# Gate rows: transposed on TensorE and sent in runs of 512 bytes, instead of scattered in runs of 4 bytes

## The chip, the cores and the metric

One core of a Trainium2 chip runs the kernel. The metric is the device time of one execution in microseconds (us). Three runs of the kernel before took 2084.08, 2084.61 and 2075.7 us, median 2084.08.

Engines: PE is TensorE (matmuls; PEld its weight loads), DVE VectorE, ACT ScalarE, POOL GpSimd, and SP the queue that issues all DMAs here.

## The reference

One decoder layer on x (256 tokens, 2048 features, float32), conditioned by one vector c of 2048.

```python
cond = silu(c)
sh1, sc1, gt1, sh2, sc2, gt2, sh3, sc3, gt3 = split(cond @ ada_w + ada_b, 9)
x = x + 0.5 * gt1 * swiglu(ada_in(x, norm_g[0], sh1, sc1), ...)      # FFN 1
x = x + gt2 * hybrid_mixer(ada_in(x, norm_g[1], sh2, sc2), ...)      # attention and delta-rule heads
x = x + 0.5 * gt3 * swiglu(ada_in(x, norm_g[2], sh3, sc3), ...)      # FFN 2
out = rmsnorm(x, final_norm)
```

`ada_in` is an RMS norm that is scaled and shifted by vectors of the nine. `swiglu(h) = (silu(h wg) * (h wu)) wd` with an inner width of 5632. The change touches only the three gate vectors `gt1`, `gt2`, `gt3` (2048 numbers each), on their way to where they multiply a row of x.

## The kernel before

**Weights.** All weight matrices are packed on the host into 5392 tiles of 128x128, in the order in which they are used, and read in 674 blocks of eight tiles (512 KB). In this text the blocks are counted from 0 in that order. For each block SP issues a load into `wraw` (L98), ACT casts it to `whi` (L100, the high part of a split of float32 into two), DVE subtracts to get `wlo` (L116, the low part), and PE multiplies with both. There are three buffers of each in the mixer, and one more of each (`more`, for every fourth block) in the FFNs. Loads therefore run ahead of casts, and casts ahead of PE, by as many blocks as there are buffers.

**Stages.** FFN 1 uses blocks 0 to 263 (gate and up projections of the first 28 of 44 column groups from block 0, their down projection from block 112, then the second part), the mixer blocks 264 to about 410, FFN 2 the rest. In a gate/up step PE accumulates into PSUM pairs `pgu`, DVE multiplies the two halves (`sg`, or `acc` in the first part), PE transposes the product (`pz`, L554, eight transposes) and ACT and DVE split it into `hid`. In a down step PE accumulates into `pd`, and `residual` (L498, L499) multiplies it with the gate row `gtr` (as `rs`) and adds it to x.

**The vectors of the conditioning.** The nine vectors are not computed by matmuls. Each column group of 128 outputs is one load of 1 MB (`adat`, L251) and one DVE instruction that multiplies it with silu(c) and sums along the row (L262, 2.35 us), into one column of the tile `mod` (128 x 160). So vector m lies in `mod` as 16 columns: number p of group j is at partition p, column 16 m + j. A table of paces (`RATE`) says how many of these sums go with each weight block.

**Gate rows.** The residual needs the gate vector along the free axis and on all partitions: `gtr`, 128 x 2048, every partition the same. Each gate vector (m = 2, 5 and 8) goes there by quarters of 512 numbers, b = 0 to 3, in two steps that are queued as soon as the fourth column of a quarter is summed (in `ada_sum`):
- `row_send` (L294): a DMA from four columns of `mod` to the DRAM tile `gd`;
- `row_load` (L300): a DMA from `gd` to all partitions of a quarter of `gtr`.

`W.after(n, f)` runs f when the program is written out n weight blocks later. With `ROW_LAG = (6, 13)` the send follows the sum by 6 blocks and the load by 13. Both wait in program order behind the newest weight load (`issue_after(W.last)`). There is one `gtr` for three gates, so a row of the next gate may be loaded only after the last residual of the current one: `gate["open"]` names the current one. Sums of gate 5 that are done while gate 2 is open queue nothing; when FFN 1 is written out, `gate_open(5)` queues all four sends 6 blocks later and all four loads 13 blocks later. `row_need` forces what is still owed before a residual. `bank` (used for `pgu`, `pd`, `pz`) hands out the eight PSUM banks in turn.

**What sets the order.** The program is written in the order of the weight blocks; a scheduler then orders each engine's instructions by its own estimate of when they become ready, so an added instruction can move others. Each engine and SP's queue run their instructions strictly in that order: what waits holds up what stands behind it.

Of the kernel before, what the change touches and what calls it, by code (L numbers as in the profile page):

```python
# [8 lines left out]
F32 = mybir.dt.float32  # L9
# [7 lines left out]
P = 128  # L17
D = 2048
T = 256
KD = D // P  # L20
# [8 lines left out]
ROW_LAG = (6, 13)  # L29
# [101 lines left out]
def layer_kernel(ctx: ExitStack, tc: tile.TileContext, xrow, c, adaw, cols, cst, fng, w, out, order, dbg=None):  # L131
    nc = tc.nc
    V, A, G, PE = nc.vector, nc.scalar, nc.gpsimd, nc.tensor
# [7 lines left out]
    tiny = ctx.enter_context(tc.tile_pool(name="tiny", bufs=2))  # L141
# [13 lines left out]
    def psn(i, name):  # L155

        i %= 8
        return psb(name) if i < N_BIG else pss(name) if i < N_BIG + N_GDN else psf(name)

    W = Stream(nc, w, raw, hi, lo)  # L160
# [10 lines left out]
    gdram = ctx.enter_context(tc.tile_pool(name="gdram", bufs=1, space=bass.MemoryType.DRAM)).tile([3, KD, P], F32, name="gd")  # L171
# [47 lines left out]
    def L(name, lo_=0, n=None):  # L219
        o, wd = COL[name]  # L220
        return colt[:, o + lo_ : o + (wd if n is None else lo_ + n)]

    ident = L("ident")

    mod = keep.tile([P, 10 * KD], F32, name="mod")
# [7 lines left out]
    def ada_col():  # L233

        i = ada_st["i"]
        if i >= len(ada_seq):
            return
        ada_st["i"] += 1
        m, j = ada_seq[i]
        if first_ada:  # L240
            t = first_ada.pop(0)
            if i >= 2:
                with tc.issue_after(W.last):
                    nc.sync.dma_start(t, adaw[i])
        else:
            t = adap.tile([P, D], F32, name="adat")
            if W.last is None:
                nc.sync.dma_start(t, adaw[i])
            else:
                with tc.issue_after(W.last):  # L250
                    nc.sync.dma_start(t, adaw[i])  # L251
        ada_open.append(lambda: ada_sum(t, m, j))
        if i < 2 * KD:
            ada_close(i)
        else:
            W.after(ADA_LAG, lambda: ada_close(i))

    def ada_sum(t, m, j):

        q = m * KD + j  # L260
        with W.behind(False):
            V.tensor_tensor_reduce(t, t, cs, HALF.get(m, 1.0), L("adab", q, 1), ALU.mult, ALU.add, mod[:, q : q + 1])  # L262
        if (m, j) in ada_done:
            ada_done[m, j]()
        if m in ROW and j % 4 == 3:
            row_owed[m, j // 4] = [row_send, row_load]
            if m == gate["open"]:
                row_soon(m, j // 4)

    def ada_close(i):  # L270

# [4 lines left out]
    ROW = {2: 0, 5: 1, 8: 2}  # L276
    row_owed, gate = {}, {"open": 2}

    def row_soon(m, b):

        for n in ROW_LAG:
            W.after(n, lambda: row_next(m, b))

    def gate_open(m):

        gate["open"] = m
        for e, b in row_owed:
            if e == m:
                row_soon(m, b)

    def row_send(m, b):

        with tc.issue_after(W.last):
            nc.sync.dma_start(gdram[ROW[m], 4 * b : 4 * b + 4].rearrange("j p -> p j"), mod[:, m * KD + 4 * b : m * KD + 4 * b + 4])  # L294

    def row_load(m, b):

# [1 line left out]
        with tc.issue_after(W.last):  # L299
            nc.sync.dma_start(gtr[:, 512 * b : 512 * b + 512], src)  # L300

    def row_next(m, b):

        if row_owed.get((m, b)):
            row_owed[m, b].pop(0)(m, b)

    def row_need(m, b):

        ada_need(m, 4 * b + 3)
        while row_owed[m, b]:  # L310
            row_next(m, b)
# [202 lines left out]
    def bank(name):  # L514

        turn[0] += 1
        return psn(turn[0], name)
# [123 lines left out]
    def ffn(which, m_sh, m_sc, m_gt, squares):  # L641
        f_ = PARTS[which]
        with tc.tile_pool(name=f"hid{which}", bufs=f_[1] // 4) as hp, \
                (nullcontext(sp_0) if which == 0 else tc.tile_pool(name=f"sg{which}", bufs=2)) as sp, \
                tc.tile_pool(name=f"more{which}", bufs=1) as more:
            W.more = (more, more, more) if MORE else None
            for half in range(2):
                if which == 0 and half == 0:
                    r = first_row
                    for j in range(KD):  # L650
                        ada_done[0, j] = lambda j=j: modulate_one(j, gains(0, 1, j, 1), mod[:, j : j + 1], r)
                    W.hold, W.held = None, [ada_done[0, 0]().ins]
                    chunks, lead, need = list(zip(CHUNKS[:-1], CHUNKS[1:])), LEAD, lambda k: ada_need(0, k)
                else:
                    if half == 0:
                        modulate(2 * which, m_sh, m_sc, hview[0])
                    chunks, lead, need = [(0, KD)], (LATER_LEAD if half == 0 else 0,), h_need
                hid = gate_up(which, f_[half], f_[half + 1], hp, sp, chunks, lead, need)
                if half and squares == "final":
                    fng_load()  # L660
                down(which, f_[half], f_[half + 1], hid, m_gt, squares if half else None)
            W.more = None
        if which == 0:
            gate_open(5)
# [72 lines left out]
    def mixer():  # L737
# [488 lines left out]
        for bs in ((0, 1), (2,), (3,)):  # L1226
# [9 lines left out]
            else:  # L1236
                for t in range(2):
                    residual(pj[3][t], t, 3, 5, "mid")
        gate_open(8)
        mx.close()  # L1240

# [131 lines left out]
```

## Time and profile before

| | |
|---|---|
| runs, us | 2084.08, 2084.61, 2075.7 |
| profiled execution, us | 2079.78 (its span 2078.0) |
| mean granted TensorE clock | 0.982 |
| FFN 1 | 0 to 784 us |
| mixer | 784 to 1320 us |
| FFN 2 and the final norm | 1320 to 2078 us |
| moved by DMA | 524.20 MB, 251 GB/s over the span |

How to read the rows below. A timeline row is: start in us from the span's start, duration, engine, line of the kernel, operation, tiles out<-in, shapes, count, and in brackets the idle time before it and what ended it. `SPq` is SP's queue; its duration is the issue, not the transfer. A matmul's own row lasts 0.39 us, but they are pipelined, 0.22 to 0.23 us apart at full clock. A row of a stretch is: from:to and its length, busy time (and instructions) of PE, PEld, DVE, ACT and POOL, the granted TensorE clock, the busy share of the DMA engines (over 1 where transfers overlap in an engine), and the GB/s moved. A wait row is: who <- whom, us in total, times, longest.

### The profile page before, as it was taken

The numbers are of one execution on the slowest core, as the hardware profiler recorded it, in microseconds if no ns is written. First come the engines' busy times: TensorE is split into PE (matmuls) and PEld (weight loads), VectorE is DVE, ScalarE is ACT, GpSimd is POOL, SyncE is SP. The second block draws the span as 40 slices with busy tenths as digits, with TensorE's granted clock in tenths as the row PEclk, the third lists the DMA queues.
The fourth block names the chain that finished last, engine by engine and source line by source line (L and its number), as shares of the span: only waits on it lengthen the run. The fifth ranks groups of instructions, "written<-read, shape, count | busy, mean of one in ns | idle before, by whom it ended". The sixth has DMA issues, their size and how long they took to land.

```text
span 2078.0 us, 25410 instructions
## 1 busy us (share of the span) xinstructions
PE 2010.1 (97%) x9372; PEld 1653.0 (80%) x9373; DVE 1487.4 (72%) x2073; ACT 993.3 (48%) x1426; POOL 2.7 (0%) x15
## 2 busy tenths in 40 slices
PE   8999999999999998999999989989999999999997
PEld 6788878777888887788878878778888888888886
DVE  7999989887877877898868866755556554455454
ACT  6544444333334446856656644644444344444443
POOL 0000000000000000000000000000000000000000
PEclk9999999999999999999999989999999999999999
DMA  9989899987888885666565556667678765555653
GB/s 364 353 319 360 307 311 317 352 354 310 326 330 335 329 298 193 205 228 205 202 225 187 187 182 243 202 183 257 219 245 256 190 220 193 193 190 189 209 192 132
DMA packets 139455, 524.20 MB, mean 252 GB/s; under 512 B 24633, under 2 KB 29881, under 8 KB 121025
## 3 DMA queue, kind: packets, MB, share of 16 engines
q1 hardware_dynamic: 139330, 522.58, 72.3%
q8 instruction: 73, 1.20, 0.2%
q14 instruction: 52, 0.43, 0.1%
HBM read 517.10 MB, written 5.41 MB: 251 GB/s over the span
## 4 chain that ended last, share of the span: by engine, by line
PE 81%; DVE 7%; DMA 6%; ACT 3%; issue 2%; SPq 0%; ACTq 0%; DVEq 0%
PE pgu L532 14%; PE pgu L535 14%; PE pgu L533 14%; PE pd L535 7%; PE pd L532 7%; PE pd L533 7%; PE pp L476 5%; DVE wlo L116 3%; DMA wraw<-in_w_dram 3%; PE pp L477 2%; DMA adat<-in_ada_dram 2%; PE po L532 1%; PE po L535 1%; PE po L533 1%; DVE adat L262 1%
## 5 line engine op out<-in xcount | busy, mean ns | idle before, releaser
L100 ACT CAST whi<-wraw 128x1024 fp32r<-128x1024 f32 x674 | 705.8, 1053 | 867.6 <-DMA wraw<-in_w_dram 321.8
L116 DVE TENSOR_TENSOR wlo<-wraw,whi 128x1024 fp32r<-128x1024 f32 x674 | 815.2, 1222 | 385.1 <-ACT whi L100 382.6
L532 PE MATMUL pgu<-whi,hs 128*128 128x512 f32 x1408 | 552.4, 394 | 10.4 <-ACT hs L382 5.8
L533 PE MATMUL pgu<-whi,hs 128*128 128x512 f32 x1408 | 549.5, 391 | 2.2 <-DVE hs L427 2.2
L535 PE MATMUL pgu<-wlo,hs 128*128 128x512 f32 x1408 | 436.3, 391 | 4.2 <-DVE wlo L116 4.0
L262 DVE CUSTOM_DVE_ANT_0 adat<-adat,cs,colt 128x2048 f32<-128x2048 f32 x140 | 328.7, 2348 | 53.7 <-DMA adat<-in_ada_dram 53.1
L532 PEld LDWEIGHTS pgu<-whi,hs 128*128 128x128 f32 x1408 | 266.3, 189 | 68.0 <-ACT hs L382 6.7
L535 PEld LDWEIGHTS pgu<-wlo,hs 128*128 128x128 f32 x1408 | 264.2, 188 | 62.5 <-DVE wlo L116 8.0
L533 PEld LDWEIGHTS pgu<-whi,hs 128*128 128x128 f32 x1408 | 266.0, 189 | 58.0 <-DVE hs L427 2.7
L532 PE MATMUL pd<-whi,hid 128*128 128x512 f32 x704 | 275.8, 392 | 1.3 <-ACT whi L100 1.3
L533 PE MATMUL pd<-whi,hid 128*128 128x512 f32 x704 | 275.1, 391 | 0.0
L476 PE MATMUL pp<-hs,whi 128*128 128x512 f32 x656 | 241.9, 405 | 1.3 <-ACT xn L414 1.1
L535 PE MATMUL pd<-wlo,hid 128*128 128x512 f32 x704 | 224.8, 392 | 6.4 <-DVE wlo L116 6.2
L477 PE MATMUL pp<-hs,wlo 128*128 128x256 f32 x656 | 188.4, 287 | 0.9 <-DVE wlo L116 0.9
L535 PEld LDWEIGHTS pd<-wlo,hid 128*128 128x128 f32 x704 | 132.2, 189 | 36.8 <-DVE wlo L116 9.6
L532 PEld LDWEIGHTS pd<-whi,hid 128*128 128x128 f32 x704 | 133.0, 189 | 29.9 <-ACT whi L100 2.2
L533 PEld LDWEIGHTS pd<-whi,hid 128*128 128x128 f32 x704 | 132.9, 189 | 27.6
L476 PEld LDWEIGHTS pp<-hs,whi 128*128 128x128 f32 x656 | 124.8, 190 | 25.6 <-ACT xn L414 1.5
L477 PEld LDWEIGHTS pp<-hs,wlo 128*128 128x128 f32 x656 | 125.2, 191 | 2.3 <-DVE wlo L116 1.4
L788 PE MATMUL pv<-wlo,hs 128*128 128x512 f32 x128 | 52.0, 406 | 2.8 <-DVE wlo L116 2.8
L789 PE MATMUL pv<-whi,hs 128*128 128x512 f32 x128 | 51.4, 401 | 0.0
L787 PE MATMUL pv<-whi,hs 128*128 128x512 f32 x128 | 51.2, 404 | 0.0
(310 smaller groups left out, 1372.4 us busy)
## 6 DMA issues: line engine op xcount, KB each, us to landing
wraw<-in_w_dram SPq DMA_DIRECT2D x674, 512.0 KB, 4.4
adat<-in_ada_dram SPq DMA_DIRECT2D x140, 1024.0 KB, 7.6
gtr<-gd SPq DMA_DIRECT2D x12, 256.0 KB, 6.7
rw<-rowd SPq DMA_DIRECT2D x24, 128.0 KB, 4.0
x<-in_xr_dram SPq DMA_DIRECT2D x4, 512.0 KB, 6.0
adaf<-in_ada_dram SPq DMA_DIRECT2D x4, 512.0 KB, 7.9
adaf<-in_ada_dram SPq DMA_DIRECT2D x2, 1024.0 KB, 12.5
xd<-x SPq DMA_DIRECT2D x4, 512.0 KB, 7.0
```

Of the source, the lines that this page charges most:

```text
L100: self.cast = self.nc.scalar.copy(self.h, r).ins
L116: nc.vector.tensor_tensor(self.l, r, self.h.bitcast(F32), ALU.subtract)
L262: V.tensor_tensor_reduce(t, t, cs, HALF.get(m, 1.0), L("adab", q, 1), ALU.mult, ALU.add, mod[:, q : q + 1])
L476: PE.matmul(ps, wt[0], act.rearrange("p a t -> p (a t)"), start=first, stop=False)
L477: PE.matmul(ps[:, :T], wt[1], act[:, 0], start=False, stop=last)
L532: PE.matmul(ps[t], hi_(t), wh, start=first, stop=False)
L533: PE.matmul(ps[t], lo_(t), wh, start=False, stop=False)
L535: PE.matmul(ps[t], hi_(t), wl, start=False, stop=last)
L787: PE.matmul(pv[t], hs[:, k, 0, sl], wh, start=(k == 0), stop=False)
L788: PE.matmul(pv[t], hs[:, k, 0, sl], wl, start=False, stop=False)
L789: PE.matmul(pv[t], hs[:, k, 1, sl], wh, start=False, stop=(k == KD - 1))
```

## The change

- A quarter is now sent in three instructions instead of one: PE transposes the four columns of `mod` into a PSUM bank (`pgr`, 4 x 128), ACT copies that to a small tile `gs` (4 x 128), and SP sends `gs` to `gd`. The DMA writes four runs of 512 B instead of 512 runs of 4 B.
- The send is queued 6 blocks after the sum for every gate, open or not. So gate 5's four sends move from the start of the mixer into FFN 1.
- The load is queued 13 blocks after the sum where the gate is open, as before; where it opens later, at 2 + b blocks after `gate_open` instead of 13.

```diff
         if m in ROW and j % 4 == 3:
             row_owed[m, j // 4] = [row_send, row_load]
+            W.after(ROW_LAG[0], lambda: row_next(m, j // 4, 2))
             if m == gate["open"]:
-                row_soon(m, j // 4)
+                row_soon(m, j // 4, ROW_LAG[1])
...
-    def row_soon(m, b):
-
-        for n in ROW_LAG:
-            W.after(n, lambda: row_next(m, b))
+    def row_soon(m, b, n):
+
+        W.after(n, lambda: row_next(m, b, 1))
 
     def gate_open(m):
 
         gate["open"] = m
         for e, b in row_owed:
             if e == m:
-                row_soon(m, b)
+                row_soon(m, b, 2 + b)
 
     def row_send(m, b):
 
+        pg = bank("pgr")
+        PE.transpose(pg[:4, :P], mod[:, m * KD + 4 * b : m * KD + 4 * b + 4], ident)
+        gs = tiny.tile([4, P], F32, name="gs")
+        A.copy(gs, pg[:4, :P])
         with tc.issue_after(W.last):
-            nc.sync.dma_start(gdram[ROW[m], 4 * b : 4 * b + 4].rearrange("j p -> p j"), mod[:, m * KD + 4 * b : m * KD + 4 * b + 4])
+            nc.sync.dma_start(gdram[ROW[m], 4 * b : 4 * b + 4], gs)
...
-    def row_next(m, b):
-
-        if row_owed.get((m, b)):
+    def row_next(m, b, left=0):
+
+        while len(row_owed[m, b]) >= max(left, 1):
             row_owed[m, b].pop(0)(m, b)
+            if not left:
+                break
```

The added lines stand ahead of most of the kernel, so line numbers after them grow by up to 6 (L498 becomes L504).

Where the instructions stand. First SP's queue near the end of FFN 1, where weight loads 235 to 240 are issued; before:

```order
L98 DMA wraw_5317<-in_w_dram 128x1024
L98 DMA wraw_5335<-in_w_dram 128x1024
L251 DMA adat_5341<-in_ada_dram 128x2048
L98 DMA wraw_5355<-in_w_dram 128x1024
L98 DMA wraw_5374<-in_w_dram 128x1024
L98 DMA wraw_5392<-in_w_dram 128x1024
L251 DMA adat_5399<-in_ada_dram 128x2048
```

and now:

```order
L98 DMA wraw_5348<-in_w_dram 128x1024
L98 DMA wraw_5371<-in_w_dram 128x1024
L251 DMA adat_5377<-in_ada_dram 128x2048
L98 DMA wraw_5391<-in_w_dram 128x1024
L298 DMA gd_91<-gs_5356 4x128
L98 DMA wraw_5410<-in_w_dram 128x1024
L98 DMA wraw_5428<-in_w_dram 128x1024
L251 DMA adat_5435<-in_ada_dram 128x2048
```

Gate 5's fourth send now stands between weight loads 237 and 238. It reads `gs_5356`, which ACT writes at this place of its own order (now; casts 235 to 238):

```order
L100 CAST whi_5350<-wraw_5348 128x1024
L100 CAST whi_5373<-wraw_5371 128x1024
L296 COPY gs_5356<-pgr_5354 4x128
L100 CAST whi_5393<-wraw_5391 128x1024
L100 CAST whi_5412<-wraw_5410 128x1024
```

The copy stands behind cast 236; on PE its transpose stands behind the last matmul of block 234. The other sends are placed alike: counted in weight blocks, the transposes of FFN 1 stand behind blocks 83, 95, 106, 118 (gate 2), 200, 208, 216, 234 (gate 5), the copies behind casts 87, 98, 110, 121, 202, 209, 218, 236, and the sends behind loads 88, 99, 111, 121, 203, 214, 224, 237. In FFN 2 these are 431, 463, 495, 527, then four casts and seven loads later.

Last, DVE around block 127, where the first residual of FFN 1 stands; before:

```order
L116 TENSOR_TENSOR wlo_3097<-wraw_3093,whi_3095 128x1024
L498 TENSOR_TENSOR rs_3101<-pd_2802,gtr_87 128x512
L498 TENSOR_TENSOR rs_3124<-pd_2803,gtr_87 128x512
L499 TENSOR_TENSOR x_85<-x_85,rs_3101 128x512
L499 TENSOR_TENSOR x_85<-x_85,rs_3124 128x512
L262 ISA adat_3104,mod_137<-adat_3104,cs_86,colt_93 128x2048
L262 ISA mod_137 128x1
L116 TENSOR_TENSOR wlo_3122<-wraw_3118,whi_3120 128x1024
```

and now:

```order
L116 TENSOR_TENSOR wlo_3113<-wraw_3109,whi_3111 128x1024
L262 ISA adat_3120,mod_137<-adat_3120,cs_86,colt_93 128x2048
L262 ISA mod_137 128x1
L504 TENSOR_TENSOR rs_3117<-pd_2814,gtr_87 128x512
L116 TENSOR_TENSOR wlo_3138<-wraw_3134,whi_3136 128x1024
L505 TENSOR_TENSOR x_85<-x_85,rs_3117 128x512
L504 TENSOR_TENSOR rs_3140<-pd_2815,gtr_87 128x512
L116 TENSOR_TENSOR wlo_3159<-wraw_3155,whi_3157 128x1024
```

The first `wlo` is that of block 126, the next that of block 127. The column sum has moved ahead of the residual, and `wlo` of block 127 ahead of the second `rs`. Beyond these places the order differs in the mixer, on all engines, from about block 275 to block 338; behind that only the added instructions do.

## The prediction

> **What bounds the kernel now.** The page's engine row and its chain come first; 0.5% of the time, about what a measurement of this kernel can tell from no change, is 10.4 us.
>
> ```profile
> PE 2010.1 (97%) x9372; PEld 1653.0 (80%) x9373; DVE 1487.4 (72%) x2073; ACT 993.3 (48%) x1426; POOL 2.7 (0%) x15
> PE 81%; DVE 7%; DMA 6%; ACT 3%; issue 2%; SPq 0%; ACTq 0%; DVEq 0%
> wraw<-in_w_dram SPq DMA_DIRECT2D x674, 512.0 KB, 4.4
> gd<-mod SPq DMA_DIRECT2D x12, 2.0 KB, 10.6
> ```
>
> TensorE is busy 97% of the span: only 68 us are not matmul, so the change can win only what stalls TensorE now. The last two rows are DMA issues with their median time to landing: a send of 2 KB takes 10.6 us, a weight block of 512 KB takes 4.4. So the next view is what the DMA engines move behind the sends (SP's timeline for their times; then stretches: PE, PEld, DVE, ACT and POOL busy, PE clock, DMA share, GB/s).
>
> ```profile
> 251.82 0.43 SPq L294 DMA_DIRECT2D gd<-mod  x1
> 286.70 0.43 SPq L294 DMA_DIRECT2D gd<-mod  x1
> 320.81 0.43 SPq L294 DMA_DIRECT2D gd<-mod  x1
> 358.13 0.43 SPq L294 DMA_DIRECT2D gd<-mod  x1
> 244.00:252.00 8.00, 8.00 (x37) 6.64 (x36) 6.93 (x7) 4.40 (x6) 0.00 (x0) 1.00 0.97 366
> 256.00:264.00 8.00, 8.00 (x41) 6.72 (x40) 8.00 (x10) 2.79 (x4) 0.00 (x0) 1.00 0.88 166
> 264.00:268.00 4.00, 4.00 (x20) 3.30 (x19) 3.60 (x6) 1.91 (x2) 0.00 (x0) 1.00 1.04 426
> 292.00:300.00 8.00, 7.47 (x33) 5.84 (x32) 4.73 (x5) 2.37 (x4) 0.00 (x0) 1.00 0.98 68
> 360.00:368.00 8.00, 8.00 (x37) 6.64 (x36) 4.60 (x5) 1.48 (x2) 0.00 (x0) 1.00 1.07 146
> ```
>
> These are the four sends of the first gate row. Some 5 us after each, for 8 us (three of the four are shown), the engines are as busy as before (share about 1) but move 68 to 166 GB/s instead of 366 to 426: loads behind a send stand still. What TensorE loses by it in this stage:
>
> ```profile
> 265.50:392.70 127.20, 123.57 (x549) 99.37 (x548) 106.80 (x111) 54.02 (x60) 0.00 (x0) 1.00 0.99 325
> 522.30:563.00 40.70, 40.70 (x182) 33.68 (x181) 32.11 (x30) 15.40 (x16) 0.00 (x0) 1.00 0.91 354
> L554 PE MATMUL pz<-colt,acc 128*128 128x128 f32 x32 | 4.4, 274 | 0.8 <-DVE acc L577 0.8
> 300.37 0.50 PE L532 MATMUL pgu<-whi,hs 128*128 128x512 f32 x1 [0.89 <-ACT whi L100]
> ```
>
> The second stretch has no send: 180 matmuls (182 less two across its edges) in 40.70 us, 0.226 each. The first holds 516 such and the 32 transposes of the third row (4.4 us): 116.7 + 4.4 = 121.1, so 127.2 - 121.1 = **6.1 us** are lost. The last row is one of these stops, for a cast that waited for its load. The clearest case is the first send of the last gate row:
>
> ```profile
> 1375.42 0.43 SPq L294 DMA_DIRECT2D gd<-mod  x1
> 1380.00:1386.50 6.50, 6.50 (x30) 5.25 (x28) 0.77 (x1) 1.05 (x1) 0.00 (x0) 1.00 0.88 36
> 1385.73 2.35 DVE L262 CUSTOM_DVE_ANT_0 adat<-adat,cs,colt 128x2048 f32<-128x2048 f32 x1 [7.99 <-DMA adat<-in_ada_dram]
> DMA to landing us min/median/max: 6.0/7.7/13.0
> 1390.48 1.12 PE L554 MATMUL pz<-colt,sg 128*128 128x128 f32 x4 [3.76 <-DVE sg L586]
> 1391.82 0.63 PE L533 MATMUL pgu<-whi,hs 128*128 128x512 f32 x1
> 1392.25 0.63 PE L532 MATMUL pgu<-whi,hs 128*128 128x512 f32 x1
> 1391.20:1397.10 5.90, 5.90 (x19) 4.74 (x18) 3.23 (x4) 1.79 (x3) 0.00 (x0) 0.55 0.81 267
> 1400.00:1700.00 300.00, 300.00 (x1345) 248.84 (x1344) 174.14 (x159) 124.17 (x129) 0.00 (x0) 1.00 0.75 233
> ```
>
> The engines move 36 GB/s; the `adat` load of that place lands after 13.0 us (the maximum of 13 in this stage, median 7.7); VectorE stands behind it for 7.99 us; TensorE waits 3.76 us for VectorE. Then it runs at clock 0.55, with matmuls 0.43 us apart: twelve of them lose 12 x 0.2 = 2.4, eight transposes about 0.7. Together **6.9 us**. The three later sends lie in the last row's stretch, in which TensorE never stops: 0.
>
> The four sends of the middle gate row go out together in the next stage's start:
>
> ```profile
> 789.15 2.08 SPq L294 DMA_DIRECT2D gd<-mod  x4
> 799.25 1.06 ACT L100 CAST whi<-wraw 128x1024 fp32r<-128x1024 f32 x1 [0.40 <-PE pp L476]
> PE pxt L417 <- ACT xn L414: 8.0, 2, 4.6
> ```
>
> The casts there wait for TensorE, not for loads, and TensorE itself for the rows of the norm (the last row: 8.0 us at the starts of two stages, this one and the last). I take their removal as 0.
>
> **The change part by part.** *Removed:* twelve sends of 512 runs. I count 6.1 + 6.9 = 13.0 us, between 0 (if something else holds those loads) and 13.0.
>
> *Added on TensorE:* twelve transposes. The trace has none with four columns; the nearest row is `pz`, 4.4 / 32 = 0.14 us. Bounds: 0 (hidden in a stop) and its unhidden length 0.27; taken 0.14 x 12 = **1.6 us**, all on the path, since TensorE is the bound.
>
> *Added on ScalarE:* twelve copies 4x128 out of PSUM.
>
> ```profile
> L1005 ACT COPY Tm<-put 64x128 f32<-64x128 f32 x8 | 2.1, 258 | 5.0 <-PE put L1048 4.9
> ```
>
> At 0.26 us they make 3.1 us on an engine that is busy 48%: 0 on the path; without that cover 3.1. Each waits for its transpose, and casts queue behind it. In the new order it stands two to four casts ahead of TensorE, about where a cast waits for a free buffer anyway: 0.
>
> *Added on SP, the risk:* a send now waits for that copy, with weight loads queued behind it. The longest hold is at the last send of the middle row (between loads 237 and 238, counted from 0, where no old send disturbs the trace):
>
> ```profile
> 696.77 7.29 SPq L98 DMA_DIRECT2D wraw<-in_w_dram  x3
> 701.39 3.91 ACT L100 CAST whi<-wraw 128x1024 fp32r<-128x1024 f32 x4
> 711.58 0.39 PE L532 MATMUL pd<-whi,hid 128*128 128x512 f32 x1
> ```
>
> The first row is loads 237, 238 and 239; the second, casts 235 to 238. The copy follows cast 236 and the transpose at the end of block 234, so at about 703.7; SP is held from 697.2 to there, about 6.5 us, and load 238 goes out at 703.9 instead of 697.9. Add 4.4 to land, 1.0 cast, 1.2 subtraction: 710.5. TensorE takes block 238 at 711.6: spare 1.1 us. By the same reckoning I estimate the first row's holds at 3 to 7 us, with no less spare. Bounds for a stop: 0, and what the stop of the next fence cost, 3.7 us; six of the eight sends in this stage have such holds, so 0 to 22. I take **2 us**, near the lower end, since the reckoning ends before TensorE. In the last stage sends stand seven loads ahead of TensorE: 0. There the row's load follows one weight load later and waits for the send to land: a hold of a landing, 4.4 us, against a lead of seven blocks of twelve matmuls, 7 x 12 x 0.226 = 19 us: 0.
>
> *Moved:* VectorE's order around block 127.
>
> ```profile
> 389.96 1.29 DVE L498 TENSOR_TENSOR rs<-pd,gtr 128x512 f32<-128x512 f32 x2 [2.98 <-PE pd L535]
> 392.37 2.35 DVE L262 CUSTOM_DVE_ANT_0 adat<-adat,cs,colt 128x2048 f32<-128x2048 f32 x1
> 394.64 2.35 DVE L116 TENSOR_TENSOR wlo<-wraw,whi 128x1024 fp32r<-128x1024 f32 x2
> 395.92 0.83 PE L535 MATMUL pd<-wlo,hid 128*128 128x512 f32 x2 [2.14 <-DVE wlo L116]
> 396.55 0.63 PE L532 MATMUL pd<-whi,hid 128*128 128x512 f32 x1
> ```
>
> Now two `rs`, two additions and a 2.35 us column sum stand between the wait and `wlo` 127; TensorE stops 2.14 us and then runs eight matmuls 0.43 apart (1.6 more): 3.7. In the new order the sum stands ahead of `rs`, in the 2.98 us of idle time, and `wlo` follows the first `rs`. Bounds: 3.7 gained, or 0 if that `adat` is late itself; taken **2.8**.
>
> The mixer's order changes too, from weight block 275 to 338 (817 to 1061 us).
>
> ```profile
> 817.00:1061.00 244.00, 237.00 (x1328) 196.12 (x1327) 207.99 (x535) 163.62 (x348) 0.67 (x4) 0.99 0.62 212
> ```
>
> TensorE idles 7.0 us there. A new order can win that, or lose about as much: taken 0, bounds -7 and +7. The middle row's four loads move ahead too, from load 276 to loads 265 to 268, where the residuals that read the old row are done or nearly so and TensorE waits for the norm: 0.
>
> *Sum*, against the profiled run's 2079.78 us (span 2078.0 and 1.8 around it): -13.0 + 1.6 + 2.0 - 2.8 = -12.2, so 2067.6. The runs shown are 2075.7, 2084.08 and 2084.61, median 2084.08; the profiled run lies between them. The mean of these four is 2081; minus 12.2 it is **2069 us**.
>
> **The rivals.** *B, the first stage keeps its loss.* SP's holds stop as many loads as the slow writes did, so of the four stalls in 265 to 393 nothing comes back and block 127 stays: -6.9 + 1.6 = -5.3, 2076. For it: the holds are 3 to 7 us, the stalls 8. Against: a held SP leaves the loads in flight alone, and the engines have shown 426 GB/s against the 354 that this stage asks for.
>
> *C, slower: SP's hold empties the weight buffers.* Place: loads 89, 100, 112, 122, 204 and 238. It decides where a load takes over 5.5 us (4.4 + 1.1) to land. Price 3.7 us a stop as at block 127: 6 x 3.7 = 22.2 + 1.6 - 13.0 = +10.8, 2092. Against: only the longest holds have so little spare.
> The Trainium skill, TensorE: Matmul & The Clock Gate, section "Part 1: The HAM clock gate", has the clock fall after an idle window of about 3.4 us; the 2.14 us stop here was followed by matmuls of 0.63 us all the same, so the measurement decides. By the page such a stop would cost 2.1 and the sum of C would be 2082.
>
> *D, run length does not matter.* The sends cost what any 2 KB write costs, and other traffic held those loads: then only +1.6, 2083. For it: the engines are at share 0.97 before a send. Against: the two stretches without a send shown here (244, 522) move 366 and 354 GB/s at that share, and every stretch shown behind one moves less than half.
> The Trainium skill, DMA: Bandwidth & Descriptors, section "Anatomy of one DMA", fits a DMA (another issue path) as about 2.0 us plus bytes at 436 GB/s, whatever its runs; an estimate by it is 2.0 us for the old send and the new alike. The trace's 10.6 does not agree.
>
> *E, the mixer's new order loses its bound:* -12.2 + 7.0 = -5.2, 2076. For it: chains of many engines cross there. Against: they are the same chains, and win as easily as lose.
>
> **How the numbers follow.** Forecast 0.63, B 0.20, C 0.06, D 0.05, E 0.06. The forecast's own range is 2061 to 2076 (its unknowns: 1.6, 2.0, 2.8 and part of the mixer's 7). Of its 0.63, 0.07 fall short of 10.4 us. Faster 0.56; same 0.07 + 0.20 + 0.05 + 0.06 = 0.38; slower 0.06. The range 2059 to 2083 takes in B, D and E.
>
> **What would show it.** Right: `gd<-gs` lands in under 5 us; no 8 us stretch under 200 GB/s behind it; no `adat` of 13 us near 1375, and neither the 3.76 us wait of `pz` nor clock 0.55 behind it; 265 to 393 some 5 us shorter; `wlo` 127 ahead of the second `rs` without a stop. Wrong: TensorE waiting for casts or `wlo` right behind a send, SP waiting for `gs` over 7 us, a mixer longer by over 6 us, `pgr` far over 0.27 us.

## The result, and the profile after

The changed kernel takes 2067.26 us (median of five runs, 2061.78 to 2067.8) against 2082.96 us of the kernel before (five runs): ratio 0.9926, 95% interval 0.9903 to 0.9948. Measured again later, on another chip, it took 2062.96 against 2082.77, ratio 0.990 (0.9876 to 0.9925). It is faster by 0.7 to 1.0%. The forecast was 2069 us, faster.

The profiled execution of the changed kernel took 2061.78 us (span 2060.0), 18.0 less than that of the kernel before. The two traces side by side: the first fence has two stretches of the kernel before, that of the first gate row's sends and the start of the last stage (PE, PEld, DVE, ACT, POOL busy, PE clock, DMA share, GB/s). The second has the page's engine row of the changed kernel and the same two stretches of it:

```profile
264.00:394.00 130.00, 126.14 (x560) 101.16 (x558) 109.20 (x112) 54.04 (x60) 0.00 (x0) 1.00 0.99 327
1375.00:1400.00 25.00, 21.24 (x86) 17.20 (x85) 11.77 (x13) 7.79 (x9) 0.00 (x0) 0.86 0.70 174
```

```profile
PE 1998.8 (97%) x9384; PEld 1647.0 (80%) x9385; DVE 1487.2 (72%) x2073; ACT 996.5 (48%) x1438; POOL 2.7 (0%) x15
...
264.00:394.00 130.00, 130.00 (x592) 107.51 (x592) 117.60 (x120) 56.47 (x65) 0.00 (x0) 1.00 0.89 337
1375.00:1400.00 25.00, 25.00 (x116) 20.55 (x115) 14.49 (x13) 11.14 (x14) 0.00 (x0) 1.00 0.70 250
```

In the same 130 us TensorE does 592 instructions instead of 560, without a stop, and at the start of the last stage the clock is 1.00 instead of 0.86.

The waits say what went. Of the kernel before (who <- whom: us in total, times, longest):

```profile
ACT whi L100 <- DMA wraw<-in_w_dram: 321.8, 182, 9.2
DVE adat L262 <- DMA adat<-in_ada_dram: 53.1, 41, 8.0
```

Of the changed kernel:

```profile
ACT whi L100 <- DMA wraw<-in_w_dram: 276.6, 163, 5.2
DVE adat L262 <- DMA adat<-in_ada_dram: 34.5, 33, 2.9
```

And SP's own waits in the changed kernel:

```profile
SPq L298 <- ACT gs L296: 46.0, 10, 9.3
SPq L304 <- DMA gd<-gs: 2.0, 2, 1.4
```

No weight load is waited for longer than 5.2 us any more (9.2 before), and no column load longer than 2.9 (8.0). In their place SP waits for the copies, 46.0 us in ten waits, up to 9.3 us, and TensorE feels almost nothing of it, as the table below shows. The last send of the middle row is one of the longer holds (SP's timeline of the changed kernel, then ScalarE's):

```profile
688.43 0.33 SPq L98 DMA_DIRECT2D wraw<-in_w_dram  x1
695.65 0.27 SPq L298 DMA_DIRECT2D gd<-gs  x1
696.01 0.80 SPq L98 DMA_DIRECT2D wraw<-in_w_dram  x2
```

```profile
695.37 0.25 ACT L296 COPY gs<-pgr 4x128 f32<-4x128 f32 x1 [0.31 <-PE pgr L294]
```

Load 238 goes out at 696.0, and TensorE needs it at 703.3.

Last, VectorE around block 127 in the changed kernel:

```profile
382.13 2.35 DVE L262 CUSTOM_DVE_ANT_0 adat<-adat,cs,colt 128x2048 f32<-128x2048 f32 x1 [1.72 <-DMA adat<-in_ada_dram]
384.77 0.69 DVE L504 TENSOR_TENSOR rs<-pd,gtr 128x512 f32<-128x512 f32 x1 [0.27 <-PE pd L541]
385.42 1.22 DVE L116 TENSOR_TENSOR wlo<-wraw,whi 128x1024 fp32r<-128x1024 f32 x1
387.16 0.68 DVE L504 TENSOR_TENSOR rs<-pd,gtr 128x512 f32<-128x512 f32 x1
```

The column sum stands ahead of `rs`, `wlo` of block 127 behind the first `rs`; TensorE does not stop there.

**Where the 18.0 us lie.** This table, for the kernel before, the changed one and the experiments below (e1 to e10 are their runs), gives the time in us from TensorE's first matmul of one weight block to that of another, worked out from each kernel's trace. It repeats within some tenths from execution to execution except where a cause sits, and in the mixer.

| blocks | 84-122 | 122-130 | 130-172 | 200-240 | 264-415 | 415-427 | 427-434 | 434-670 |
|---|---|---|---|---|---|---|---|---|
| what lies there | first row's sends | block 127 | two more residuals | middle row's new sends | mixer | start of FFN 2 | last row's first send | the other three |
| before | 113.6 | 25.8 | 122.7 | 112.3 | 551.3 | 37.1 | 26.8 | 649.6 |
| changed | 107.6 | 21.8 | 122.7 | 113.3 | 550.3 | 34.7 | 20.1 | 650.0 |
| changed, again | 107.6 | 21.8 | 122.7 | 113.3 | 553.3 | 34.7 | 20.1 | 650.1 |
| e1: old form, new times | 123.4 | 24.3 | 122.7 | 123.5 | 556.0 | 35.8 | 26.7 | 649.6 |
| e2: 512 B, no work added | 107.5 | 25.8 | 122.8 | 112.3 | 554.6 | 35.8 | 20.0 | 649.6 |
| e3: runs of 16 B | 107.3 | 24.2 | 122.8 | 112.3 | 550.3 | 36.6 | 20.0 | 649.6 |
| e5: sends by ScalarE | 107.6 | 21.7 | 122.8 | 112.7 | 547.2 | 34.7 | 20.2 | 650.0 |
| e6: 16 B, strided read | 107.3 | 26.5 | 125.1 | 112.3 | 550.7 | 35.5 | 20.1 | 649.5 |
| e7: changed, residual behind | 107.9 | 21.9 | 114.3 | 113.3 | 552.2 | 34.7 | 20.2 | 649.9 |
| e8: e6, residual behind | 107.2 | 21.7 | 114.3 | 112.3 | 550.9 | 35.6 | 20.0 | 649.6 |
| e10: before, residual behind | 123.9 | 21.7 | 114.3 | 112.3 | 542.7 | 35.7 | 26.3 | 649.6 |

Before to changed: -6.0 at the first row's sends, -4.0 at block 127, -6.7 at the last row's first send, -2.4 at the start of FFN 2, -1.0 in the mixer; +1.0 at the middle row's sends, +0.4 at the last three, and +0.7 elsewhere: -18.0.

### The profile page after: what moved, and what is told of

Read it like the earlier page. It is cut to its first block, busy times and chain, and to the rows that moved or that the text cites. A ratio compares the mean times of both kernels' runs of the same rounds, so it can differ in the third digit from the quotient of the medians.

```text
span 2060.0 us, 25445 instructions
## 1 busy us (share of the span) xinstructions
PE 1998.8 (97%) x9384; PEld 1647.0 (80%) x9385; DVE 1487.2 (72%) x2073; ACT 996.5 (48%) x1438; POOL 2.7 (0%) x15
## 4 chain that ended last, share of the span: by engine, by line
PE 88%; DVE 5%; DMA 3%; ACT 2%; issue 1%; SPq 0%; ACTq 0%; DVEq 0%
PE pgu L541 15%; PE pgu L538 15%; PE pgu L539 15%; PE pd L541 8%; PE pd L539 8%; PE pd L538 8%; PE pp L482 5%; PE pp L483 3%; DVE wlo L116 2%; DMA adat<-in_ada_dram 2%; PE po L538 1%; PE po L539 1%; PE po L541 1%; PE pv L794 1%; PE pv L793 1%; PE pv L795 1%
```

## The experiments

Two questions: is it the runs of 4 B that hold the loads, or when and how the sends go out? And what do the added transposes, copies and holds cost?

**1. The old form at the new times** (e1; changed kernel).

```diff
-        pg = bank("pgr")
-        PE.transpose(pg[:4, :P], mod[:, m * KD + 4 * b : m * KD + 4 * b + 4], ident)
-        gs = tiny.tile([4, P], F32, name="gs")
-        A.copy(gs, pg[:4, :P])
         with tc.issue_after(W.last):
-            nc.sync.dma_start(gdram[ROW[m], 4 * b : 4 * b + 4], gs)
+            nc.sync.dma_start(gdram[ROW[m], 4 * b : 4 * b + 4].rearrange("j p -> p j"), mod[:, m * KD + 4 * b : m * KD + 4 * b + 4])
```

> The changed kernel with the old send (512 runs of 4 B from mod, no transpose, no copy), at the new times: the middle row's four sends go out singly in FFN 1. If the 4 B runs are the cost, about 6 us come back in 264 to 394 us and 7 us at the first send of FFN 2, and VectorE, whose order around block 127 is that of before again, gives back 3.7 us; 1.6 us of transposes and 0.8 us of holds go: 2067 + 13 + 3.7 - 2.4 = 2081, and up to 6 us more if the four middle sends cost there what the first four cost. If the times at which the sends go out carried the gain, and not the length of the runs, 2064 to 2067.

Measured: 2097.67 us, ratio to the kernel before 1.0063 (1.0029 to 1.0098). Slower than before, and 10 us above the 2087 that I had as the most, so the new times alone carry no gain: they are a loss with the old form. The middle row's four sends, which went out together at 789 us at no cost, now go out singly in FFN 1 and cost 11.2 us (123.5 against 112.3). Stretches behind two of them (issued at 610.4 and 679.2), with the rates of the kernel before's sends:

```profile
616.00:622.00 6.00, 5.53 (x29) 4.42 (x28) 5.64 (x7) 2.02 (x3) 0.00 (x0) 1.00 0.32 39
685.00:691.00 6.00, 6.00 (x28) 4.80 (x26) 1.68 (x2) 0.00 (x0) 0.00 (x0) 1.00 1.37 89
```

39 and 89 GB/s; behind the other two it is 125 and 232. The first row's sends cost 15.9 us in this execution (123.4 against the 107.5 of experiment 2), where they had cost 6.1 in the profiled one of the kernel before. That was outside the bounds I had. The profiled execution, 2105.61 us, is the longest of the five.

**2. Runs of 512 B and nothing added** (e2; kernel before, same order on all engines).

```diff
-            nc.sync.dma_start(gdram[ROW[m], 4 * b : 4 * b + 4].rearrange("j p -> p j"), mod[:, m * KD + 4 * b : m * KD + 4 * b + 4])
+            nc.sync.dma_start(gdram[ROW[m], 4 * b : 4 * b + 4], colt[:4, :P])
```

> The kernel before, in its own order on every engine, but each send takes 4 x 128 numbers that lie in SBUF since the start (part of colt) and writes four runs of 512 B: no transpose, copy or wait is added, and the gate rows hold other numbers (that part of the output is left out). If the 4 B runs are the cost: 13 us less, 2068, with the stop of 3.7 us at block 127 still there if VectorE's order makes it (and 2064, without it, if the adat load there was late by the sends). If the run length does not matter: no change, 2079 to 2083.

Measured: 2067.64 us, ratio 0.9915 (0.9885 to 0.9944), on a chip where the kernel before took 2086.13: 18.5 less. The order of every engine is that of the kernel before, and so the send itself is the cause. It differs in the length of its runs and in where its numbers come from; experiment 3 keeps the old source, and that leaves the runs. Stretches 6 to 12 us behind the four sends of the first row, of this kernel:

```profile
261.00:267.00 6.00, 6.00 (x32) 5.06 (x31) 6.00 (x7) 2.37 (x5) 0.00 (x0) 1.00 0.93 309
295.00:301.00 6.00, 6.00 (x28) 4.99 (x27) 6.00 (x6) 4.23 (x5) 0.00 (x0) 1.00 0.88 338
324.00:330.00 6.00, 6.00 (x28) 4.97 (x27) 5.10 (x7) 2.11 (x2) 0.00 (x0) 1.00 0.64 241
361.00:367.00 6.00, 6.00 (x28) 4.99 (x27) 5.80 (x6) 2.11 (x2) 0.00 (x0) 1.00 1.00 409
```

and the same behind those of the kernel before:

```profile
258.00:264.00 6.00, 6.00 (x32) 5.05 (x31) 6.00 (x7) 1.07 (x2) 0.00 (x0) 1.00 0.56 141
293.00:299.00 6.00, 6.00 (x28) 4.99 (x27) 3.73 (x4) 0.64 (x2) 0.00 (x0) 1.00 0.67 44
327.00:333.00 6.00, 6.00 (x32) 5.07 (x31) 2.62 (x3) 0.00 (x0) 0.00 (x0) 1.00 0.73 79
364.00:370.00 6.00, 5.71 (x25) 4.10 (x23) 1.82 (x2) 1.05 (x1) 0.00 (x0) 1.00 0.62 137
```

241 to 409 GB/s instead of 44 to 141. Block 127 still takes 25.8: that stop is VectorE's order and no late load.

**3. Runs of 16 B** (e3; kernel before, same order on all engines).

```diff
-            nc.sync.dma_start(gdram[ROW[m], 4 * b : 4 * b + 4].rearrange("j p -> p j"), mod[:, m * KD + 4 * b : m * KD + 4 * b + 4])
+            nc.sync.dma_start(gdram[ROW[m], 4 * b : 4 * b + 4].rearrange("j p -> (j p)").rearrange("(p j) -> p j", j=4), mod[:, m * KD + 4 * b : m * KD + 4 * b + 4])
```

> The kernel before in its own order on every engine, but the four columns of a quarter are written as 128 runs of 16 B, one from each partition, so the gate rows hold their numbers in another order (their right order is left out). If each short write costs the same, a quarter of the stretch of 8 us is left, 2 us, which the buffers mostly hide: 2068 to 2071, near the time with four runs of 512 B. If it is the reading from 128 partitions, or any write under 512 B, that holds the engines, 2077 to 2083.

Measured: 2063.72 us, ratio 0.9908 (0.9877 to 0.994): as good as runs of 512 B, and a little under the 2068 to 2071 expected. Neither the 128 partitions that are read nor a length under 512 B is what holds the loads.

**4. The sends issued by ScalarE** (e5; changed kernel), twice, the second time beside the changed kernel on one chip.

```diff
-        with tc.issue_after(W.last):
-            nc.sync.dma_start(gdram[ROW[m], 4 * b : 4 * b + 4], gs)
+        nc.scalar.dma_start(gdram[ROW[m], 4 * b : 4 * b + 4], gs)
```

> The changed kernel with its twelve sends issued by ScalarE right behind the copy, not by SP: no weight load waits for a copy any more. If the holds on SP cost what the trace of the changed kernel shows at the middle row's sends (0.8 us at block 217), 2066, not to be told from the changed kernel; if they cost the 2 us that the prediction took, 2065; if the issue on ScalarE holds up casts, 2068 to 2071.

> The changed kernel with its sends issued by ScalarE, beside the changed kernel: 1 us faster if only the stop of block 217 goes (0.9 us in its trace), 7 us faster if the holds on SP cost more than that in other executions.

> The changed kernel once more, beside the next three on one chip: 2061 to 2068, a ratio to the kernel before of 0.990 to 0.995. If the sends by ScalarE were faster by 7 us (2060 against 2067) only because they ran on another day than the changed kernel, this one comes out near 2060 here too.

Measured: first 2059.95 us, ratio 0.9882 (0.9855 to 0.9909), which looked like 7 us gained; beside the changed kernel 2063.84 (0.9883 to 0.9927) against its 2062.96 (0.9876 to 0.9925). So the 7 us lay between chips or executions, not in the queue. In the trace, 200-240 is 0.6 us shorter (112.7 against 113.3): of two stops of 0.36 us, right behind the transposes in blocks 200 and 216, the second is gone. The 46 us for which SP waits in the changed kernel cost well under 1 us there; the medians can't tell them from nothing.

**5. Runs of 16 B with the right result** (e6; kernel before, send as in 3).

```diff
-        V.tensor_tensor(d, ps, gtr[:, sl], ALU.mult)
+        V.tensor_tensor(d.rearrange("q (j p) -> q j p", j=4), ps.rearrange("q (j p) -> q j p", j=4), gtr[:, sl].rearrange("q (p j) -> q j p", j=4), ALU.mult)
```

> The kernel before in its own order on every engine, the quarter sent as 128 runs of 16 B, and the residual reading the gate row with a stride of four numbers, so that the result is right again without any transpose, copy or wait: as the 128 runs of 16 B measured, 2060 to 2068, with the stop at block 127 still there. If the strided read makes rs slower than 0.65 us each, up to 5 us more over the eight places where TensorE waits behind it.

Measured: 2072.68 us, ratio 0.9947 (0.9927 to 0.9966). The strided read is not free. The group of `rs` with the plain read (runs of 16 B) and with the strided one (this kernel):

```profile
L498 DVE TENSOR_TENSOR rs<-pd,gtr 128x512 f32<-128x512 f32 x32 | 21.2, 688 | 41.8 <-PE pd L535 41.8
```

```profile
L498 DVE TENSOR_TENSOR rs<-pd,gtr 128x512 f32<-128x512 f32 x32 | 33.3, 1064 | 39.3 <-PE pd L535 39.3
```

1064 ns instead of 688. In the order of the kernel before, `wlo` stands behind these, so TensorE's stops get longer: it adds 2.3 us in 130-172, and 0.7 in 122-130 (26.5 against the 25.8 of e2). The 24.2 of e3 there is lower by 1.6 more because TensorE's clock did not fall behind that stop, as the last section shows.

**6. Each residual held behind the next subtraction**, on the kernel of 5 (e8), on the changed kernel (e7) and on the kernel before (e10). The edit is shown on the changed kernel.

```diff
-                nc.vector.tensor_tensor(self.l, r, self.h.bitcast(F32), ALU.subtract)
+                self.sub = nc.vector.tensor_tensor(self.l, r, self.h.bitcast(F32), ALU.subtract).ins
...
-        V.tensor_tensor(d, ps, gtr[:, sl], ALU.mult)
+        with tc.issue_after(W.sub):
+            V.tensor_tensor(d, ps, gtr[:, sl], ALU.mult)
...
-            W.after(n + 1, lambda ps=ps, t=t, b=b: residual(ps, t, b, m_gt, squares))
+            W.after(n + 2, lambda ps=ps, t=t, b=b: residual(ps, t, b, m_gt, squares))
```

> The last one, and each residual is queued one weight block later and held behind that block's subtraction on VectorE: no pair of rs, additions and column sum stands ahead of a wlo any more. If that order makes the stops, those at blocks 127 (3.7 us), 140 to 142 (2.0), 155 (3.9) and 169 (2.4) go: 10 to 12 us less than the last one, about 2052. If TensorE then waits for the PSUM banks that come free a block later, or the late loads made the stops, no gain.

> The changed kernel with each residual queued one weight block later and held behind that block's subtraction. The stops at blocks 140 to 142, 155 and 169, where VectorE still has two rs, two additions and a column sum ahead of a wlo, go: 2.0 + 3.9 + 2.4 = 8.3 us, so 2063 - 8 = 2055. If those stops come from late loads, no change: 2063.

> The kernel before with nothing but that order of the residuals, its sends still in 512 runs of 4 B: 3.7 + 2.0 + 3.9 + 2.4 = 12 us less, 2083 - 12 = 2071, if the two causes add up. If the slow sends are what makes wlo of block 127 late, 2074 to 2083.

Measured: 2051.22 us (ratio 0.9845, 0.9824 to 0.9867) for the kernel of 5 with it; 2054.76 (0.984, 0.9806 to 0.9875) for the changed kernel with it; 2070.17 (0.9915, 0.9885 to 0.9945) for the kernel before with it alone. All three came within 1 us of the time expected. In each, 130-172 falls to 114.3 and 122-130 to 21.7 or 21.9. For the changed kernel that is 8.3 us in 122-172, as expected. The other two hits are in part luck. The kernel of 5 gained 21 us, where 10 to 12 were expected; 15.6 of them lie in 122-172, where the strided read had made the stops longer. The kernel before gained 16 by the medians of one chip, where 12 were expected: 12.5 lie in 122-172, and in its trace the mixer is 8.6 us shorter (542.7) and the first row's sends 10.3 dearer (123.9). The kernel of 5 with the same order has 550.9 in the mixer, so that part is not the order's. Order and run length are two separate causes that add up: on one chip -16 us for the order on the kernel before, and another 15 for the new sends on top of it. Both 2051 and 2055 beat the two kernels of this case. The other chance, that late loads make these stops, fell: with the slow writes left in, the stops go as well.

**7. Which short runs hold the loads?** Kernel of 2 and, behind each send of the first and the last gate row, one more write to an unused tensor (`to` is a piece of it). The first kernel (e9) has four forms, the same in both rows; the second (e11) has eight.

```diff
...
+            if m != 5:
+                to = gd2[ROW[m] // 2 * 4 + b]
+                if b == 0:
+                    nc.sync.dma_start(to[:P].rearrange("(p e) -> p e", e=1), colt[:, 0:1])
+                elif b == 1:
+                    nc.sync.dma_start(to[: 512 * 4].rearrange("(k p e) -> p k e", k=4, e=4), colt[:, :16].rearrange("p (k e) -> p k e", e=4))
+                elif b == 2:
+                    nc.sync.dma_start(to[: 512 * 64].rearrange("(k p e) -> p k e", k=4, e=64)[:, :, 0:1], colt[:, :4].rearrange("p (k e) -> p k e", e=1))
+                else:
+                    nc.sync.dma_start(to[: 512 * 16].rearrange("(k p e) -> p k e", k=4, e=16), colt[:, :64].rearrange("p (k e) -> p k e", e=16))
```

```diff
...
+                n, w, gap = {(2, 0): (32, 1, 1), (2, 1): (128, 2, 2), (2, 2): (128, 1, 4), (2, 3): (128, 1, 16),
+                             (8, 0): (128, 1, 1), (8, 1): (64, 1, 1), (8, 2): (128, 1, 8), (8, 3): (128, 4, 4)}[m, b]
+                nc.sync.dma_start(to[: n * gap].rearrange("(p e) -> p e", e=gap)[:, :w], colt[:n, :w])
```

> The kernel before with sends in 512 B runs of numbers that lie ready (the gate rows' own numbers are left out), and behind each send of the first and the last gate row one more write to an unused tensor: behind the first 128 runs of 4 B, the second 512 runs of 16 B, the third 512 runs of 4 B that lie 256 B apart, the fourth 512 runs of 64 B. If each short run costs the same, whatever its length, the loads stand still for 2, 8, 8 and 8 us behind them; if the length decides, the second and the fourth hold less than the third; if it is that the runs share 2 KB of DRAM, the third holds nothing. Against the kernel with the same sends and no further write (2068), each 8 us stretch costs about 1.5 us in FFN 1.

> Again the kernel before with 512 B sends of numbers that lie ready (the gate rows' own numbers are left out) and one more write behind each send of the first and last gate row. First row: 32 runs of 4 B side by side; 128 runs of 8 B side by side; 128 runs of 4 B, 16 B apart; 128 runs of 4 B, 64 B apart. Last row: 128 runs of 4 B side by side; 64 of them; 128 of 4 B, 32 B apart; 128 runs of 16 B side by side. If short runs that share a piece of DRAM are written one after another (8 us for 128 of 4 B, 0.06 us each), the side-by-side ones hold the loads for 2 us (32), up to 8 us (8 B), 8 us, 4 us (64) and up to 8 us (16 B), those 64 B apart for nothing, and 16 and 32 B apart tell how large the piece is. If 4 B is special, only the 4 B runs hold, at any distance; but 256 B apart they did not.

One run each, on two other chips, where the kernel before took 2086.33 (median of seven) and 2073.97 (one run): 2068.24 and 2066.83 us (2067.64 for the kernel of 2; the added writes also move the order in the mixer, which these stretches lie ahead of). Stretches 6 to 12 us behind the four sends of the first row, for the first kernel (128 runs of 4 B side by side; 512 of 16 B; 512 of 4 B, 256 B apart; 512 of 64 B):

```profile
260.00:266.00 6.00, 6.00 (x32) 5.08 (x31) 6.00 (x7) 1.50 (x3) 0.00 (x0) 1.00 0.78 105
296.00:302.00 6.00, 6.00 (x28) 4.99 (x27) 5.74 (x6) 2.62 (x4) 0.00 (x0) 1.00 0.94 303
325.00:331.00 6.00, 6.00 (x30) 4.97 (x29) 5.82 (x7) 1.01 (x1) 0.00 (x0) 1.00 0.73 271
362.00:368.00 6.00, 6.00 (x28) 4.99 (x27) 5.11 (x5) 2.00 (x3) 0.00 (x0) 1.00 1.02 406
```

and for the second (32 runs of 4 B side by side; 128 of 8 B side by side; 128 of 4 B, 16 B apart; 128 of 4 B, 64 B apart):

```profile
259.00:265.00 6.00, 6.00 (x32) 5.07 (x31) 6.00 (x7) 1.47 (x4) 0.00 (x0) 1.00 0.85 218
293.00:299.00 6.00, 6.00 (x28) 4.99 (x27) 4.76 (x5) 2.14 (x4) 0.00 (x0) 1.00 0.71 204
323.00:329.00 6.00, 6.00 (x32) 5.01 (x31) 6.00 (x7) 0.64 (x1) 0.00 (x0) 1.00 0.88 348
360.00:366.00 6.00, 6.00 (x29) 4.95 (x28) 4.58 (x5) 1.42 (x2) 0.00 (x0) 1.00 0.99 398
```

The first form holds the loads as the old sends did, with a quarter of their runs: 105 GB/s where the kernel without it moves 309. 32 runs of 4 B and 128 of 8 B hold them in part (218 and 204). 512 runs of 16 or 64 B do not, and neither do runs of 4 B that lie 16, 64 or 256 B apart (348, 398 and 271, against 241 to 409 at these places without any further write). So it is neither the count of runs nor their length alone: it is short runs side by side, closer than 16 B. That each short run costs the same fell, and so did "4 B is special at any distance". Each stretch is one reading, but the single packets of the traces agree. In the 12 us behind the send the longest packet of a load took 5.1 us at 128 runs of 4 B side by side, 3.5 at 32, 4.3 at 128 of 8 B, and at most 2.0 behind the other forms of the first row and behind the sends of the kernel of 2. In the last row the 128 runs of 4 B hold a packet for 5.6 and 5.4 us again, and 64 of them for 2.1, where the kernel of 2 has 1.1 at most. There, where loads are sparser, the forms 32 B apart and of 16 B could not be told from no write. No distance between 8 and 16 B was tried.

## Why the prediction was right, and where not

**The 13.0 us of the sends: right in the profiled execution.** The 6.1 of the first row measured 6.0 (113.6 to 107.6), the 6.9 at 1375 us 6.7 (26.8 to 20.1), and the three later sends 0, as said. Runs of 512 B alone, with everything else in place, give the same 107.5 and 20.0. But "between 0 and 13.0" was a bound taken from one execution. The same sends at the same places cost 15.9 and 16.4 us in the traces of e1 and e10, and the kernel before lost 18.5 us against e2 by the medians. The profiled execution was one of the kernel's milder ones; the step that failed is the upper bound of this term: 13.0 was the loss of one execution, and the sends can cost more than that.

**Transposes, 1.6 us: about right.** One lasts 0.271 us; in 434-670 three of them cost 0.4, so 0.14 each, as taken from `pz`. In 84-122 there are three (the first row's first one stands ahead of block 84), and they cost 0.1.

**SP's holds, 2.0 us: too much.** The longest is 9.3 us (the middle row's first send), not 6.5, and past the 7 us that I had named as a sign of being wrong. They cost 1.0 us with the transposes of the middle row's sends, 0.4 to 0.6 without. The estimate ended before TensorE by 1.1 us at load 238. TensorE took that block at 703.3, and its cast stood at 699.3: the load of 696.0 had landed by then, 3.3 us after its issue and not 4.4.

**Block 127, -2.8: 4.0.** The upper bound (3.7) was the right choice, and the reason for taking less was not: the `adat` load there was not late, and e2 shows the stop without slow writes, e10 its end with them. What the bound took for granted is the slow clock behind the stop, 1.6 of the 3.7. In e1 and e3 the same stop stands without it and costs 2.4 us (24.2 or 24.3 against 21.8), and so the price of 3.7 that rival C uses for a stop holds only where the clock falls.

**The mixer, 0:** 551.3 to 550.3 and 553.3. Other kernels in the order of before range from 550.3 to 554.6.

**Not foreseen, -2.4 at block 420.** TensorE stopped 2.24 us there in the kernel before, behind a column sum whose `adat` load came late (VectorE idle 2.31 us). In both traces of the changed kernel, and in e5 and e7, which were made from it, it does not. The kernels in the order of before, without the slow writes, keep about half of the loss (35.5 to 36.6 against 34.7), and so does e10 with them (35.7). What the order moves there I did not separate.

**The rivals.** B (the first stage keeps its loss) fell: 84-122 is as short as with no work added. C (SP's hold empties the buffers) fell by e5: the holds were longer than thought, and the buffers covered them all the same. D (run length does not matter) fell by e2; yet its doubt was half right, since at 16 B or at a distance run length does not matter either. E fell with the mixer's 550.3.

**How the send lands.** SP's timeline of the changed kernel at the first send of FFN 2:

```profile
1382.20 0.28 SPq L298 DMA_DIRECT2D gd<-gs  x1
1383.30 0.34 SPq L98 DMA_DIRECT2D wraw<-in_w_dram  x1
1383.69 0.42 SPq L304 DMA_DIRECT2D gtr<-gd  x1
```

The row's load, which needs what the send wrote, goes out 1.5 us behind it without a wait; at the third and the fourth send of that row it waits 0.6 and 1.4 us and goes out 2.0 and 2.9 us behind. The old form landed after 10.6 (median).
The Trainium skill, DMA: Bandwidth & Descriptors, section "Anatomy of one DMA", has a fixed cost of about 2.0 us for a DMA, on another issue path: the new send agrees roughly, with its 1.5 to 2.9, and the old form does not.

**The size.** The sum gave 2067.6 for a profiled run; that run took 2061.78, since block 127 and block 420 gave 3.6 us more than taken, the holds 1.4 less, and the rest is the mixer and what lies outside these terms. The change forecast, -12.2 us, was too small: it measured -18.0 between the profiled executions, and -15.7 and -19.8 between the medians. That the time of 2069 came within 2 us of the median of 2067.26 is luck, because its base (2081) was low by 2.

## What to carry to other kernels

Before a tile is scattered in 4 B runs, look at the GB/s 5 to 13 us behind that DMA, not at its own landing: here a write of 512 B held the loads to 105 GB/s for 6 us where 309 moved without it. It need not become long runs: here 16 B, one run from each partition, was enough, and the send needed no engine. But the row then arrives in another order, and reading it in the right one took VectorE 1064 ns a time instead of 688. And two residuals ahead of the next weight's subtraction on an in-order engine cost nearly as much as all the slow writes; holding them back by one block was worth 8, 16 and 21 us in three kernels by the medians (8.3, 12.5 and 15.6 in the stretch where they stand).

## What the runs showed of the hardware

- 128 writes of 4 B side by side (512 B in all) held the other loads about as much (105 GB/s over 6 us) as 512 of them in four rows of 512 B did (44 to 141); 32 of 4 B and 128 of 8 B held them about half as much (218 and 204); 512 writes of 16 B, or 4 B at 16 B or more from one another, did not. Why the neighbourhood decides isn't shown.
- The two weaker holds of experiment 7 cost TensorE nothing (84-122 is 107.3 us in that kernel), the full one 1.3 us (108.8 in the other, against 107.5; TensorE stops there once, 1.12 us). The four old sends of the first row cost 6.1, 15.9 or 16.4 us in three executions; what decides between these stays open.
- A VectorE multiply of 128x512 with one operand out of SBUF at a stride of four numbers took 1064 ns, and 688 with a stride of one.
- Behind one and the same stop TensorE's clock fell in one kernel and not in another. At block 127 e2 and e3, with the same order on every engine, both stop 2.14 us. The row of the stop and the stretch behind it, the clock in the third last column, first of e2:

```profile
392.52 1.22 PE L535 MATMUL pd<-wlo,hid 128*128 128x512 f32 x2 [2.14 <-DVE wlo L116]
392.50:396.70 4.20, 4.18 (x11) 3.35 (x12) 4.20 (x4) 0.00 (x0) 0.00 (x0) 0.59 0.86 328
```

and of e3:

```profile
389.84 0.73 PE L535 MATMUL pd<-wlo,hid 128*128 128x512 f32 x2 [2.14 <-DVE wlo L116]
389.80:394.00 4.20, 4.16 (x18) 3.47 (x19) 4.20 (x4) 0.00 (x0) 0.00 (x0) 1.00 0.89 335
```

11 matmuls instead of 18 in 4.2 us: the slow clock is the 1.6 us between 25.8 and 24.2 in 122-130.
- In the kernel before the clock fell after a stop of 2.14 us (at 393 us) and not after one of 2.24 us (at 1357 us). Stretches behind the two stops and the row of the second stop:

```profile
395.00:399.20 4.20, 3.28 (x9) 2.58 (x10) 4.20 (x5) 2.10 (x2) 0.00 (x0) 0.67 0.83 285
1359.40:1363.00 3.60, 3.53 (x16) 2.93 (x17) 2.79 (x7) 2.87 (x4) 0.00 (x0) 1.00 0.59 174
```

```profile
1359.47 0.50 PE L533 MATMUL pgu<-whi,hs 128*128 128x512 f32 x1 [2.24 <-DVE hs L427]
```

So the length of the stop alone doesn't set it. What does isn't shown here.
